# The low half of each weight block by an accumulating transfer instead of a subtraction

## The chip, the cores and the metric

The kernel runs on one core of a Trainium2 chip. The metric is device time in microseconds (us) of one execution. The kernel before takes 1822.1 us, the median of two runs (1822.0 and 1822.19).

## The reference

Two layers of a transformer trunk on one sequence of 512 tokens with 1024 features, all in float32. A layer is a gated feed-forward block (width 2816), a mixer, and a second gated feed-forward block:

```python
for l in range(DEPTH):                                   # DEPTH = 2
    h = rms_norm(x, ffn1_norm[l])
    x = x + 0.5 * swiglu(h, ffn1_w_gate[l], ffn1_w_up[l], ffn1_w_down[l])
    h = rms_norm(x, mix_norm[l])
    proj = h @ w_in[l]                                   # q, k, v, u of 512 columns each
    ...                                                  # 4 heads of differential attention; 4 pooling groups
    x = x + jnp.concatenate([o, p], axis=-1) @ w_out[l]
    h = rms_norm(x, ffn2_norm[l])
    x = x + 0.5 * swiglu(h, ffn2_w_gate[l], ffn2_w_up[l], ffn2_w_down[l])
return rms_norm(x, final_norm)
```

Nearly all of the arithmetic is products of activations with weights that are used once per layer.

## The kernel before, in words

**Products in three parts.** Each float32 operand is held as two matmul-type (fp32r) tiles: a rounded "hi" and the remainder "lo". `mm3` (L84 to L87) makes one 128x128 by 128x512 product from three matmuls on TensorE: hi by hi (L85), hi weight by lo activation (L86), lo weight by hi activation (L87). The lo part of the weights is therefore first needed by the third matmul of a group.

**Weights.** `plan` lists all weight blocks in the order of use: 128 partitions by up to 2048 columns, up to 1 MB. `load_next` (L107) loads a block from DRAM by one transfer that SyncE's queue issues (L111) into `wraw`, of which there are two. Then `split` (L103) cuts it in halves ("tiles" below: 1024 columns each, 768 or 640 in the down projections, 256 for the pooling weights): ScalarE casts a tile to `whi` (L104), VectorE subtracts `whi` from `wraw` and writes `wlo` (L105). There are five `whi` and five `wlo` buffers; each is free again when TensorE has read the tile for the last time. `weights()` asks for the block behind the one about to be used. The first block of all goes another way: `first_project` (L612) loads it by rows and splits it in 128-column pieces.

**Order of the work.** Each engine runs its instructions in a fixed order that a scheduler has made from the program. TensorE runs through the projections of a feed-forward block in 1024-column tiles, 24 matmuls per tile (8 k tiles of three), then through the down projections (15 or 18 matmuls per tile), then the mixer, where steps of attention stand between quarters of projections. VectorE and ScalarE also carry the gating (`silu`, `up`, `hhi`, `hlo`), rope, softmax and the norms. GpSimd (POOL) only adds squares (`ssum`, L184, L201), raises to powers (`rT`, L231) and scales the rope tables (L370, L371).

Of the kernel before, what the change touches and what calls it, by code (L numbers as in the profile page):

```python
# [15 lines left out]
ALU = mybir.AluOpType  # L16
# [5 lines left out]
L = 2  # L22
# [10 lines left out]

# columns of the packed small parameters
C_F1 = 0
# [6 lines left out]

# columns of the constants that depend on shapes alone
K_COS = 0
# [4 lines left out]

# the dimensions of a head: those that rope pairs lie 16 apart in 32 partitions  # L50
ROPE_ORDER = np.arange(HD).reshape(2, 2, 16).transpose(1, 0, 2).reshape(-1)
ROPE_SWAP = [(i + 16) % 32 for i in range(32)]

# the quarters of the mixer's projections before which attention's and pooling's steps stand
S_AT = ((3, 4, 6, 8), (10, 11, 13, 15), (19, 20, 23, 25), (26, 26, 28, 29))
Y_AT = (23, 30)
# how many quarters behind their first part the others stand
LAG_Q, LAG_U, LAG_T, LAG_A, LAG_H, V_AT = 2, 2, 2, 3, 3, 14
# [3 lines left out]
def trunk(ctx: ExitStack, tc: tile.TileContext, xT, gu1, dn1, win_qk, win_v, win_u, poolw, wout, gu2, dn2, small, lams, consts, outT):  # L62
    nc = tc.nc
# [24 lines left out]

# [1 line left out]
    plan = []  # L90
# [10 lines left out]
    loaded = []  # L101

    def split(hi, lo, raw):  # L103
        nc.scalar.copy(hi, raw)  # L104
        nc.vector.tensor_sub(lo, raw, hi.bitcast(F32))  # L105

    def load_next(i):  # L107
        src, part = plan[i]
        n = src.shape[-1]
        raw = wpool.tile([P, WSLOT], F32, name="wraw", bufs=2)  # L110
        nc.sync.dma_start(raw[:, :n], src)  # L111
        parts = []
        for o in range(0, n, part):
            hi = wpool.tile([P, 1024], F32R, name="whi", bufs=5)
            lo = wpool.tile([P, 1024], F32R, name="wlo", bufs=5)
            split(hi[:, :part], lo[:, :part], raw[:, o : o + part])
            parts.append((hi, lo))
        loaded.append(parts)

    used = [0]  # L120

    def weights():
        """The next block of weights; the one behind it is loaded."""
        i = used[0]
        used[0] += 1
        while len(loaded) < min(i + 2, len(plan)):
            load_next(len(loaded))
        return loaded[i]

    # the tensor engine's clock rises with its load: it works until the first data are there  # L130
    warm = cpool.tile([P, P], BF16, name="warm")
# [4 lines left out]

# [1 line left out]
    x = cpool.tile([P, KD, S], F32, name="x")  # L138
# [9 lines left out]
    nc.vector.memset(ones, 1.0)  # L148
    # the table of functions comes in before the first data
    early = sml.tile([P, 1], F32, name="early", bufs=1)  # L150
# [4 lines left out]
    class Norm:  # L155
        """x * gain split in two, tile by tile, and the sum of the squares."""

# [31 lines left out]
    class Final:  # L189
        """x * gain in place, and the sum of the squares."""  # L190

# [26 lines left out]
    def rms_cols(sq, inv_n, tiles=range(4), pin=False):  # L218
        """1 / sqrt(mean of the squares over the partitions): tokens on the partitions."""
        ps = bank("ps_ms")  # L220
        for t in tiles:
            mm = nc.tensor.matmul(ps[:, t : t + 1], sq[:, t * P : (t + 1) * P], ones[:, 0:1], start=True, stop=True)
            if pin and t == tiles[0]:
                in_order(mm)
        return rsqrt_mean(ps, inv_n, slice(tiles[0], tiles[-1] + 1))
# [8 lines left out]
    def rms_rows(rT, tiles=range(4)):  # L234
        """The same, for all tokens on every partition."""
        n = len(tiles)
        ts = slice(tiles[0] * P, (tiles[-1] + 1) * P)
        b = single("rb")
        nc.vector.tensor_copy(b[:, ts].rearrange("p (t c) -> p t c", t=n), rT[:, tiles[0] : tiles[-1] + 1].unsqueeze(2).broadcast_to([P, n, P]))
        ps = bank("ps_r")  # L240
        for t in tiles:
            nc.tensor.transpose(ps[:, t * P : (t + 1) * P], b[:, t * P : (t + 1) * P], ident)
        r = single("r")
        nc.scalar.copy(r[:, ts], ps[:, ts])
        return r
# [7 lines left out]
    def project(norm, done):  # L253
        """Two column tiles of a projection of the normed x; yields between quarters."""
        parts = weights()
        for i in range(2):
            ps = bank("ps_pr")
            hi, lo = parts[i]
            for k in range(KD):
                c = slice(k * P, (k + 1) * P)  # L260
                mm3(ps, hi[:, c], lo[:, c], *norm.k(k), k == 0, k == KD - 1)
                if k == 3:
                    yield
            done(i, ps)
            yield
# [5 lines left out]
    def ffn(norm, l, nxt, first=None):  # L271
# [3 lines left out]
        def gated():  # L275
            """silu(gate) * up of the column tiles that stand in PSUM, split in two."""
            while r is not None and todo:
                j, i, ps = todo.pop(0)
                if i == 0:
                    s = single("silu")  # L280
                    nc.vector.tensor_mul(s, ps, r)  # L281
                    nc.scalar.activation(s, s, AF.Silu)  # L282
                    st[j] = s
                    continue
                u = single("up")
                nc.vector.tensor_mul(u, ps, r)  # L286
                if j % 2 == 0:
                    hh.append(arena("hhi"))
                    hl.append(arena("hlo"))
                hi, lo = hh[-1][:, j % 2, :], hl[-1][:, j % 2, :]  # L290
                nc.vector.tensor_mul(u, u, st.pop(j))  # L291
                nc.scalar.copy(hi, u)  # L292
                nc.vector.tensor_sub(lo, u, hi.bitcast(F32))  # L293

        st = {}
        for hf, (j0, nj) in enumerate(HALVES):
            hh, hl = [], []
            for j in range(nj):

                def done(i, ps, j=j):  # L300
                    todo.append((j, i, ps))
                    gated()

                work = first(done) if first and r is None and j == 0 else project(norm, done)
                if r is None and j == 1:
                    # the norm's factors, while the projections go on
                    next(work)
                    next(work)
                    rT = rms_cols(norm.ssum, 1.0 / D, pin=True)
                    next(work)  # L310
                    r = rms_rows(rT)
                    gated()
                run(work)
# [11 lines left out]
            last = hf == 1 and isinstance(nxt, Final)  # L325
# [4 lines left out]
            if last:  # L330
                # the last two column tiles by halves of the tokens: the first half leaves under the second
                n = KD - 2
# [14 lines left out]
    def mix(norm, l, nxt):  # L347
        st = {}

        def qk_project(h):  # L350
            """Queries (scaled) and keys of a head, with rope."""
            sw, t = pair32("sw"), pair32("t")
# [24 lines left out]
        def qk_split(h, t):  # L377
            # per map, on the two halves of the partitions: queries (hi, lo) on keys (lo, hi), in turn for the maps
            qs, ks, kf = arena("qs"), arena("ks"), arena("kf")
# [10 lines left out]
        def v_project():  # L390
            """The values, with the tokens on the partitions."""
            parts = weights()
            parts = parts + weights()
# [25 lines left out]
        def scores(h, qt):  # L419
            """The two maps for 128 queries and their difference, before the division by the first map's sum."""  # L420
            q, k, kf = st["qk", h]
# [23 lines left out]
        def turn(h, qt):  # L445
            """That difference with the keys on the partitions."""
            a = st["a", h, qt]
# [10 lines left out]
        def attend(h, qt):  # L458
            """128 queries of a head's output, on the partitions, and the sum of their squares."""
            at = st["at", h, qt]  # L460
# [31 lines left out]
        def u_project(pair):  # L492
            dh, dl = arena("dhi"), arena("dlo")

            def done(i, ps):
# [12 lines left out]
                nc.vector.scalar_tensor_tensor(df, cur, 1.0 / w, u, ALU.mult, ALU.subtract)  # L508
                # the first tokens see fewer positions
                e = sml.tile([P, 16], F32, name="edge")  # L510
# [32 lines left out]
        def out_work():  # L543
            """The output projection: pool groups and heads in the order in which they are ready."""
            ps, parts = [], []
# [31 lines left out]

        # the steps of attention and pooling stand between the quarters of the projections
        events = []
# [32 lines left out]
    def first_project(done):  # L612
        """The first block: weights and x come in by rows, and are used as they come."""
        src = plan[0][0].rearrange("p (i k n) -> p i k n", i=2, k=KD)
# [30 lines left out]

    # -lam per layer, on every partition
    nlam, subg = [], []
# [111 lines left out]
```

## Time and profile before

| | |
|---|---|
| runs | 1822.0 and 1822.19 us, median 1822.1 |
| span of the profiled execution, first to last instruction | 1818.8 us |
| TensorE matmul / weight load busy | 1801.7 us (99%) / 1480.6 us (81%) |
| VectorE busy | 919.1 us (51%) |
| ScalarE busy | 630.0 us (35%) |
| GpSimd busy | 85.2 us (5%) |
| SyncE's DMA queue | 169.17 MB, 26.4% of the 16 DMA engines' span |

The page gives no time of its own for the profiled execution beside the span; the median of the runs is 3.3 us above the span. A matmul's busy time is modelled and overlaps that of the next one, so the pace of TensorE is read from the distance between starts. "Idle before, releaser" names what an engine waited for. A transfer's time to landing runs from its issue to its completion.

### The profile page before, as it was taken

The numbers are of one execution on the slowest core, as the hardware profiler recorded it, in microseconds if no ns is written. First come the engines' busy times: TensorE is split into PE (matmuls) and PEld (weight loads), VectorE is DVE, ScalarE is ACT, GpSimd is POOL, SyncE is SP. The second block draws the span as 40 slices with busy tenths as digits, with TensorE's granted clock in tenths as the row PEclk, the third lists the DMA queues.
The fourth block names the chain that finished last, engine by engine and source line by source line (L and its number), as shares of the span: only waits on it lengthen the run. The fifth ranks groups of instructions, "written<-read, shape, count | busy, mean of one in ns | idle before, by whom it ended". The sixth has DMA issues, their size and how long they took to land.

```text
span 1818.8 us, 19923 instructions
## 1 busy us (share of the span) xinstructions
PE 1801.7 (99%) x8152; PEld 1480.6 (81%) x8152; DVE 919.1 (51%) x1350; ACT 630.0 (35%) x975; POOL 85.2 (5%) x66
## 2 busy tenths in 40 slices
PE   8999999999999999999999999999999999999997
PEld 7888888877788888888888888888777888888886
DVE  6443344477975443444444434444779644434433
ACT  6222232445553322222432222324445433222232
POOL 0000000110020000000100000002000200000001
PEclk9999999999999999999999999999999999999999
DMA  6222321322122222322322232223122222232221
GB/s 228 93 76 90 116 110 61 105 92 73 49 93 96 111 72 96 113 93 73 123 106 93 70 116 98 102 64 131 47 73 73 96 96 104 70 121 93 86 85 62
DMA packets 31805, 170.48 MB, mean 94 GB/s; under 512 B 3425, under 2 KB 8033, under 8 KB 17505
## 3 DMA queue, kind: packets, MB, share of 16 engines
q1 hardware_dynamic: 31568, 169.17, 26.4%
q8 instruction: 64, 1.05, 0.2%
q14 instruction: 29, 0.23, 0.0%
q10 hardware_dynamic: 144, 0.03, 0.0%
HBM read 167.09 MB, written 2.10 MB: 93 GB/s over the span
## 4 chain that ended last, share of the span: by engine, by line
PE 96%; DVE 2%; issue 1%; SPq 1%; DMA 0%; POOL 0%; ACT 0%; POOLq 0%; DVEq 0%; ACTq 0%
PE ps_pr L85 19%; PE ps_pr L87 19%; PE ps_pr L86 19%; PE ps_dn L86 9%; PE ps_dn L85 9%; PE ps_dn L87 9%; PE ps_wo L85 2%; PE ps_wo L87 2%; PE ps_wo L86 2%; PE ps_s L430 1%; PE ps_s L431 1%; PE ps_v L85 1%; PE ps_v L87 1%; PE ps_v L86 1%; PE ps_o L466 1%
## 5 line engine op out<-in xcount | busy, mean ns | idle before, releaser
L104 ACT CAST whi<-wraw 128x1024 fp32r<-128x1024 f32 (+4 forms) x370 | 338.5, 919 | 939.0 <-PE ps_pr L86 409.3
L85 PE MATMUL ps_pr<-xhi,whi 128*128 128x512 f32 x1600 | 626.8, 392 | 3.0 <-ACT whi L104 3.0
L87 PE MATMUL ps_pr<-xhi,wlo 128*128 128x512 f32 x1600 | 623.2, 389 | 0.5 <-DVE wlo L105 0.5
L86 PE MATMUL ps_pr<-xlo,whi 128*128 128x512 f32 x1600 | 622.9, 389 | 0.0
L105 DVE TENSOR_TENSOR wlo<-wraw,whi 128x1024 fp32r<-128x1024 f32 (+4 forms) x370 | 396.3, 1074 | 185.9 <-ACT whi L104 185.7
L85 PEld LDWEIGHTS ps_pr<-xhi,whi 128*128 128x128 f32 x1600 | 300.7, 188 | 65.5 <-ACT whi L104 4.2
L87 PEld LDWEIGHTS ps_pr<-xhi,wlo 128*128 128x128 f32 x1600 | 300.3, 188 | 63.9 <-DVE wlo L105 1.0
L86 PEld LDWEIGHTS ps_pr<-xlo,whi 128*128 128x128 f32 x1600 | 300.5, 188 | 61.3 <-DVE xlo L174 0.6
L85 PE MATMUL ps_dn<-hhi,whi 128*128 128x512 f32 (+1 forms) x724 | 277.5, 383 | 0.0
L87 PE MATMUL ps_dn<-hhi,wlo 128*128 128x512 f32 (+1 forms) x724 | 277.4, 383 | 0.0
L86 PE MATMUL ps_dn<-hlo,whi 128*128 128x512 f32 (+1 forms) x724 | 277.4, 383 | 0.0
L286 DVE TENSOR_TENSOR up<-ps_pr,r 128x512 f32<-128x512 f32 x88 | 60.8, 691 | 274.3 <-PE ps_pr L87 274.3
L85 PEld LDWEIGHTS ps_dn<-hhi,whi 128*128 128x128 f32 x724 | 136.1, 188 | 26.8
L86 PEld LDWEIGHTS ps_dn<-hlo,whi 128*128 128x128 f32 x724 | 136.1, 188 | 26.6
L87 PEld LDWEIGHTS ps_dn<-hhi,wlo 128*128 128x128 f32 x724 | 136.1, 188 | 26.6
L281 DVE TENSOR_TENSOR silu<-ps_pr,r 128x512 f32<-128x512 f32 x88 | 60.8, 691 | 174.2 <-PE ps_pr L87 171.0
L323 DVE SCALAR_TENSOR_TENSOR x<-ps_dn,x 128x512 f32<-128x512 f32 (+1 forms) x66 | 44.6, 676 | 137.1 <-PE ps_dn L87 137.1
L184 POOL TENSOR_TENSOR ssum<-ssum,sq 128x512 f32<-128x512 f32 x35 | 53.5, 1529 | 1048.5 <-ACT sq L181 1048.1
L292 ACT CAST hhi<-up 128x512 fp32r<-128x512 f32 x88 | 54.8, 624 | 76.0 <-DVE up L291 76.0
L293 DVE TENSOR_TENSOR hlo<-up,hhi 128x512 fp32r<-128x512 f32 x88 | 60.2, 687 | 17.2 <-ACT hhi L292 17.2
L291 DVE TENSOR_TENSOR up<-up,silu 128x512 f32<-128x512 f32 x88 | 60.5, 690 | 6.2 <-ACT whi L104 0.5
L282 ACT ACTIVATE silu<-silu 128x512 f32<-128x512 f32 x88 | 55.2, 628 | 3.6 <-DVE silu L281 2.9
(118 smaller groups left out, 1104.3 us busy)
## 6 DMA issues: line engine op xcount, KB each, us to landing
wraw<-gu SPq DMA_DIRECT2D x87, 1024.0 KB, 4.8
wraw<-dn1a SPq DMA_DIRECT2D x16, 768.0 KB, 4.3
wraw<-dn2a SPq DMA_DIRECT2D x16, 768.0 KB, 4.3
wraw<-dn1b SPq DMA_DIRECT2D x16, 640.0 KB, 3.9
wraw<-dn2b SPq DMA_DIRECT2D x16, 640.0 KB, 3.8
wraw<-wqk SPq DMA_DIRECT2D x8, 1024.0 KB, 4.7
wraw<-wo SPq DMA_DIRECT2D x8, 1024.0 KB, 4.8
wraw<-wv SPq DMA_DIRECT2D x4, 1024.0 KB, 4.8
```

The source lines that it names most:

```text
L85: nc.tensor.matmul(out, a_hi, b_hi, start=start, stop=False)
L86: nc.tensor.matmul(out, a_hi, b_lo, start=False, stop=False)
L87: nc.tensor.matmul(out, a_lo, b_hi, start=False, stop=stop)
L104: nc.scalar.copy(hi, raw)
L105: nc.vector.tensor_sub(lo, raw, hi.bitcast(F32))
L184: (nc.vector if first else nc.gpsimd).tensor_add(self.ssum, self.ssum, sq)
L281: nc.vector.tensor_mul(s, ps, r)
L282: nc.scalar.activation(s, s, AF.Silu)
L286: nc.vector.tensor_mul(u, ps, r)
L291: nc.vector.tensor_mul(u, u, st.pop(j))
L292: nc.scalar.copy(hi, u)
L293: nc.vector.tensor_sub(lo, u, hi.bitcast(F32))
```

## The change

For every block but the first, the lo tile is no longer subtracted by VectorE. ScalarE multiplies the raw tile by -1 into `wlo`, which rounds it as the cast does, and GpSimd's queue issues a transfer that reads the same weights from DRAM once more and adds them to `wlo` in place. The cast to `whi` stands behind these two in the program. `split` remains for the first block. Comments are removed, and the kernel's lines behind L116 stand three lower.

```diff
         for o in range(0, n, part):
             hi = wpool.tile([P, 1024], F32R, name="whi", bufs=5)
             lo = wpool.tile([P, 1024], F32R, name="wlo", bufs=5)
-            split(hi[:, :part], lo[:, :part], raw[:, o : o + part])
+
+            nc.scalar.mul(lo[:, :part], raw[:, o : o + part], -1.0)
+            nc.gpsimd.dma_start(lo[:, :part], src[:, o : o + part], accum_op=ALU.add)
+            nc.scalar.copy(hi[:, :part], raw[:, o : o + part])
             parts.append((hi, lo))
```

The first place is ScalarE near the start, where the first whole blocks are split (`sq` are squares for the norm, `r` its factor). Before:

```order
L178 ACTIVATE ssum<-x 128x512
L181 ACTIVATE sq<-x 128x512 x3
L104 CAST whi<-wraw 128x1024 x2
L181 ACTIVATE sq<-x 128x512 x4
L104 CAST whi<-wraw 128x1024 x4
L244 COPY r<-ps_r 128x512
```

Now:

```order
L181 ACTIVATE ssum<-x 128x512
L184 ACTIVATE sq<-x 128x512 x3
L117 ACTIVATE wlo<-wraw 128x1024
L119 CAST whi<-wraw 128x1024
L117 ACTIVATE wlo<-wraw 128x1024
L119 CAST whi<-wraw 128x1024
L184 ACTIVATE sq<-x 128x512 x4
L117 ACTIVATE wlo<-wraw 128x1024
```

Each cast has a multiplication ahead of it, on the same engine.

The second place is ScalarE in the middle of a feed-forward block (`silu` and `hhi` belong to the gating). Before:

```order
L282 ACTIVATE silu<-silu 128x512
L104 CAST whi<-wraw 128x1024
L292 CAST hhi<-up 128x512
L104 CAST whi<-wraw 128x1024
L282 ACTIVATE silu<-silu 128x512
```

Now:

```order
L285 ACTIVATE silu<-silu 128x512
L119 CAST whi<-wraw 128x1024
L117 ACTIVATE wlo<-wraw 128x1024
L295 CAST hhi<-up 128x512
L119 CAST whi<-wraw 128x1024
L117 ACTIVATE wlo<-wraw 128x1024
```

Here the cast goes first and the multiplication follows it.

The third place is GpSimd, from its first work to the start of the first mixer. Before:

```order
masks.py:199 AFFINE_SELECT ident<-ident 128x128
L231 TENSOR_TENSOR rT<-ms,nhalf 128x4
L184 TENSOR_TENSOR ssum<-ssum,sq 128x512 x7
L231 TENSOR_TENSOR rT<-ms,nhalf 128x4
L370 TENSOR_TENSOR cosr<-cst,r 128x512
```

Now:

```order
masks.py:199 AFFINE_SELECT ident<-ident 128x128
L118 DMA wlo<-gu 128x1024 x4
L234 TENSOR_TENSOR rT<-ms,nhalf 128x4
L118 DMA wlo<-gu 128x1024 x18
L118 DMA wlo<-dn1a 128x768 x16
L118 DMA wlo<-gu 128x1024 x20
L118 DMA wlo<-dn1b 128x640 x9
L187 TENSOR_TENSOR ssum<-ssum,sq 128x512
L118 DMA wlo<-dn1b 128x640 x2
```

GpSimd's queue now holds 354 transfers, one per tile, among the additions and powers that it had.

## Rows read from the trace of the kernel before

**Rows 1.** The page's head and part 1: span, busy time, share, instructions.

```profile
span 1818.8 us, 19923 instructions
...
PE 1801.7 (99%) x8152; PEld 1480.6 (81%) x8152; DVE 919.1 (51%) x1350; ACT 630.0 (35%) x975; POOL 85.2 (5%) x66
```

**Rows 2.** Busy time by windows; the first line names the columns.

```profile
core 0: us, PE busy (x) PEld busy (x) DVE busy (x) ACT busy (x) POOL busy (x), PEclk, DMA share, GB/s
0.00:20.00 20.00, 15.90 (x82) 12.46 (x82) 12.16 (x34) 13.96 (x32) 0.70 (x6) 1.00 0.87 283
...
200.00:300.00 100.00, 100.00 (x443) 82.80 (x442) 44.50 (x53) 28.51 (x35) 0.00 (x0) 1.00 0.25 92
450.00:470.00 20.00, 18.73 (x93) 14.79 (x92) 18.51 (x48) 10.97 (x25) 3.00 (x2) 1.00 0.00 0
1340.00:1360.00 20.00, 19.45 (x105) 16.21 (x104) 16.32 (x39) 10.11 (x23) 3.00 (x2) 1.00 0.15 53
1360.00:1380.00 20.00, 19.28 (x90) 15.09 (x91) 19.41 (x45) 10.11 (x24) 0.00 (x0) 1.00 0.17 59
1800.00:1818.00 18.00, 8.83 (x70) 8.14 (x68) 7.94 (x18) 3.53 (x8) 1.40 (x2) 0.79 0.35 117
```

**Rows 3.** Part 4 of the page: the chain that ended last, by engine.

```profile
PE 96%; DVE 2%; issue 1%; SPq 1%; DMA 0%; POOL 0%; ACT 0%; POOLq 0%; DVEq 0%; ACTq 0%
```

**Rows 4.** Timeline of TensorE and ScalarE in the first output projection: start, us.

```profile
525.02 2.00 ACT L104 CAST whi<-wraw 128x1024 fp32r<-128x1024 f32 x2 [1.51 <-PE ps_wo L86]
...
526.87 0.39 PE L85 MATMUL ps_wo<-cath,whi 128*128 128x512 f32 x1
...
532.31 0.39 PE L85 MATMUL ps_wo<-cath,whi 128*128 128x512 f32 x1
...
532.77 0.39 PE L87 MATMUL ps_wo<-cath,wlo 128*128 128x512 f32 x1
```

**Rows 5.** Timeline of ScalarE's casts in the first layer's second down half.

```profile
322.48 0.73 ACT L104 CAST whi<-wraw 128x640 fp32r<-128x640 f32 x1 [2.66 <-PE ps_dn L86]
...
325.89 0.73 ACT L104 CAST whi<-wraw 128x640 fp32r<-128x640 f32 x1 [1.25 <-PE ps_dn L86]
...
329.28 0.73 ACT L104 CAST whi<-wraw 128x640 fp32r<-128x640 f32 x1 [2.66 <-PE ps_dn L86]
```

**Rows 6.** Groups of instructions by shape: count, busy us, mean ns, idle before, releaser.

```profile
L105 DVE TENSOR_TENSOR wlo<-wraw,whi 128x1024 fp32r<-128x1024 f32 x222 | 276.9, 1249 | 77.7 <-ACT whi L104 77.5
L105 DVE TENSOR_TENSOR wlo<-wraw,whi 128x768 fp32r<-128x768 f32 x64 | 61.3, 958 | 67.1 <-ACT whi L104 67.1
L105 DVE TENSOR_TENSOR wlo<-wraw,whi 128x640 fp32r<-128x640 f32 x64 | 52.5, 820 | 41.1 <-ACT whi L104 41.1
L105 DVE TENSOR_TENSOR wlo<-wraw,whi 128x256 fp32r<-128x256 f32 x4 | 1.6, 409 | 0.0
L104 ACT CAST whi<-wraw 128x1024 fp32r<-128x1024 f32 x222 | 232.7, 1052 | 585.7 <-PE ps_pr L86 299.8 <-issue 180.5 <-PE ps_dn L86 90.6
L184 POOL TENSOR_TENSOR ssum<-ssum,sq 128x512 f32<-128x512 f32 x35 | 53.5, 1529 | 1048.5 <-ACT sq L181 1048.1
```

**Rows 7.** Part 3 of the page: SyncE's DMA queue, packets, MB, share of engines.

```profile
q1 hardware_dynamic: 31568, 169.17, 26.4%
```

**Rows 8.** Transfers by line: count, KB each, median us from issue to landing.

```profile
wraw<-gu SPq DMA_DIRECT2D x87, 1024.0 KB, 4.8
wraw<-dn1b SPq DMA_DIRECT2D x16, 640.0 KB, 3.9
cst<-consts SPq DMA_DIRECT2D x1, 584.0 KB, 8.8
wraw<-pw SPq DMA_DIRECT2D x4, 128.0 KB, 2.0
```

**Rows 9.** Line 111's issues on SyncE's queue: minimum, median, maximum ns.

```profile
L111 SPq DMA_DIRECT2D wraw<-gu x87: 327/328/599, 10.6 to 1704.9; - x87
```

**Rows 10.** Timeline where TensorE first uses a whole block.

```profile
18.44 1.99 ACT L104 CAST whi<-wraw 128x1024 fp32r<-128x1024 f32 x2 [1.13 <-DMA wraw<-gu]
19.52 2.36 DVE L105 TENSOR_TENSOR wlo<-wraw,whi 128x1024 fp32r<-128x1024 f32 x2 [0.94 <-ACT whi L104]
...
20.80 0.50 PE L87 MATMUL ps_pr<-xhi,wlo 128*128 128x512 f32 x1 [0.53 <-DVE wlo L105]
```

## The prediction

> **What bounds the kernel now.** I read the page's head first. TensorE is busy 1801.7 of 1818.8 us; no other engine is above 51% [rows 1]. The windows then say where its 17.1 us of idle time lie. In a stretch of a feed-forward block, 200 to 300 us, TensorE has no gap at all; 4.1 us are lost in the first 20 us, 9.2 us in the tail from 1800 us, and some 2.5 us in three windows of the two mixers, where VectorE is busy 16.3 to 19.4 of 20 us [rows 2]. The chain of waits agrees: 96% TensorE, 2% VectorE [rows 3]. So VectorE, which the change relieves, bounds almost nothing.
>
> TensorE's pace is to be read from starts: in the output projection one 1024-column tile takes from 526.87 to 532.31, 5.44 us for 24 matmuls or 0.227 us each [rows 4]. A 640-column tile is 15 matmuls, 3.40 us, and the casts of that stretch indeed follow each other at 3.40 us (322.48, 325.89, 329.28), each ended by TensorE, not by a transfer [rows 5]. This is the row that matters most: the preparation of weights runs as far ahead as the five buffers let it, and then waits for TensorE. A new tile can be begun when TensorE leaves the oldest one, with four others still to be used: 4 x 5.44 = 21.8 us of cover for 1024-column tiles, 4 x 3.40 = 13.6 us for 640.
>
> **The change, part by part.** *Removed:* 222 + 64 + 64 + 4 = 354 subtractions of 276.9 + 61.3 + 52.5 + 1.6 = 392 us on VectorE [rows 6], which falls from 919 to 527 us. None of it stands before TensorE except in the mixer windows above. There at most the 2.5 us of idle time come back, and at least nothing, because ScalarE, which serves the same softmax steps, receives a multiplication nearly as long (1.05 for 1.25 us). I take half, -1.3 us.
>
> *Added on ScalarE:* 354 multiplications. They have the shapes of the casts, so I price them as casts: 222 x 1.05, 64 x 0.73 for 640 columns, and 64 x 0.89, midway, for 768: 337 us [rows 5, 6]. ScalarE goes from 630 to 967 us, 53%. In a feed-forward tile that is about one extra us in 5.44; its casts spend their time waiting for TensorE, so this is covered.
>
> *Added on the DMA engines:* the bytes of 354 tiles once more: 222 x 0.524 + 64 x 0.393 + 64 x 0.328 + 4 x 0.131 = 163 MB. The queue that moves 169.17 MB takes 26.4% of the engines [rows 7]; as plain loads the new ones would take 25.5%, together 52%. The trace has no accumulating transfer. From below it cannot be cheaper than a plain load of its size: 512 KB land in 3.4 us, between 128 KB in 2.0 and 640 KB in 3.9. From above I take the slowest landing of about this size, 584 KB in 8.8 us while other loads ran [rows 8]. The value that I use is 4.8 us, the row of a 1024 KB load, since 512 KB of weights and 512 KB of destination have to be read. The Trainium skill ("Collectives: The Full Stack", Part 3) says that a reducing transfer reads two sources per chunk and so runs at about half the rate of a copying one; by it, as an estimate, the new queue would take 51% rather than 25.5% of the engines, and the first tile below would come 1.4 us later than by the plain row. No run here shows it yet.
>
> *Added on GpSimd:* 354 issues. SyncE's queue spends 0.33 us on one (0.60 at most) [rows 9]; GpSimd's own additions take 1.53 us [rows 6]. Between these, 117 to 542 us on an engine that is busy 85: covered. Its queue runs in order, so a transfer behind an `ssum` addition waits for that addition, and this for the square and the finished down tile. In the down stage that addition belongs to a tile used two blocks before the one being prepared, whose own buffer is not free earlier, so nothing is late.
>
> *Moved waits.* The new chain for a tile is cast, multiplication, transfer. For 640 columns: 0.73 + 0.73 + 8.8 = 10.3 us at the upper bound, inside the 13.6 of cover; for 1024: 1.05 + 1.05 + 8.8 = 10.9 in 21.8. Hidden. `wraw` is now released by ScalarE rather than VectorE, at about the same time.
>
> Two places have less cover. *The first whole block:* it lands at 18.44; TensorE's first matmul with its lo tile starts at 20.80, held by the subtraction [rows 10]. Now the multiplication goes first: 18.44 + 1.05 + landing = 22.9, 24.3 or 28.3, thus +2.1, **+3.5** or +7.5 us. The second tile, multiplied by 21.6, lands at 26.4, before TensorE asks at 24.3 + 5.4. *The output projection:* its four early tiles are held until the last head is done. The cast at 525.02 waits for TensorE, and the lo tile is needed at 532.77 [rows 4]. Cast and multiplication end at 527.1; landing at 530.5, 531.9 or 535.9: 0, **0** or +3.1 us, once per layer.
>
> Sum: 1818.8 + 3.5 + 0 - 1.3 = 1821.0 us of span. The median of the runs is 3.3 us above the span, so 1824 us. Without any cost at the start and with all of the mixer's idle time back it would be 1819; with the upper bounds, 1822.1 + 7.5 + 2 x 3.1 = 1836.
>
> **Rivals.** *A: the DMA engines become the bound, slower.* If an accumulating byte costs m plain bytes, the share is 26.4% + 25.5% x m, which passes 100% at m = 2.9. Then the loads no longer keep ahead, ScalarE waits for `wraw` instead of for TensorE, and the time follows the share: m = 3 gives 1.029 x 1818.8 + 3.3 = 1875, m = 4 gives 1.284 x 1818.8 + 3.3 = 2339 us. For it: in the first 20 us, with plain loads alone, the engines reach 0.87 [rows 2]. Against it: reading twice as much explains m = 2, not 3.
>
> *B: GpSimd or the latency becomes the bound, slower.* If the time L from free buffer to landed tile exceeds the cover, five buffers give one tile per (L + use) / 5. At L = 17 us a 640-column tile comes every 4.08 instead of 3.40 us (64 x 0.68 = 44) and a 768-column one, 18 matmuls, every 4.22 instead of 4.08 (64 x 0.14 = 9): 1875. At L = 20 it is 64 x 1.28 + 64 x 0.74 = 129 us: 1951. The 2% are passed near L = 16.3. The same bound appears if GpSimd needs over 3.4 us per issue. For it: no row shows what such an issue costs, and the queue is in order. Against it: L is 10.3 with my upper landing.
>
> *C: the relief of VectorE is worth more than the start costs.* Then 1818 to 1822. A gain of over 2% is nearly excluded: TensorE's 1801.7 us of busy time and 3.3 us around the span make 1805, and 2% less than now is 1786.
>
> *D: the output changes but not the work.* That the transfers don't appear at all is excluded by the order of GpSimd's instructions.
>
> **Numbers.** The forecast, everything hidden but the start, 0.66; A 0.15; B 0.15; C 0.03; a larger gain 0.01. The predicted time is the first: 1824 us. The range begins at 1818, C's end, and reaches to 1930: it takes in the upper bounds (1836), A up to m = 3.1 and B up to about L = 19. Left out are A beyond (0.11), B beyond (0.07) and 0.02 below. 2% (1786 and 1858) is what a measurement here can tell: faster 0.01, same 0.69, slower 0.30.
>
> **What would show it.** Right: TensorE without a gap in the feed-forward stretches, ScalarE's instructions on `wlo` and `whi` still ended by TensorE, a DMA share of 50 to 80%, and one gap of some 3 us more near 20 us. Start wrong: `wlo`'s transfer from issue to landing other than 4.8 us. A: DMA share at 0.9 in the feed-forward windows, ScalarE waiting for `wraw`. B: TensorE waiting for `wlo` at L87 mostly in the 640- and 768-column stretches, with GpSimd's queue busy or its landings over 13 us. What would make the prediction wrong above all is the price of the accumulating transfer, the one thing that no row here shows.

## The result and the profile after

The changed kernel takes 1843.7 us, the median of runs from 1842.5 to 1844.9, against 1822.1 before: a ratio of 1.012, 95% interval 1.0091 to 1.015. It is slower by some 22 us: clear of the scatter, but within the 2% inside which the prediction speaks of the same time. Times here and below are medians; one execution each of two experiment kernels, of 4662 us (the plain copy, whose only trace this is) and 5683 us (the mixer alone), is left out. The profiled execution has a span of 1840.8 us, 22.0 more than before [rows 1].

The page of the changed kernel: span, busy times, the two DMA queues (packets, MB, share of the 16 engines' span) and the chain that ended last.

```profile
span 1840.8 us, 20900 instructions
...
PE 1810.7 (98%) x8152; PEld 1485.5 (81%) x8152; DVE 552.8 (30%) x996; ACT 918.3 (50%) x1329; POOL 385.3 (21%) x420
...
q0 software_dynamic: 50976, 163.08, 50.3%
q1 hardware_dynamic: 31568, 169.17, 30.4%
...
PE 92%; DMA 3%; DVE 2%; issue 1%; POOL 1%; SPq 0%; ACT 0%; POOLq 0%; DVEq 0%; ACTq 0%
```

VectorE lost 366 us of work and ScalarE gained 288, and neither moved the end. The new queue q0 takes 50.3% of the engines' span for about as many bytes as the old one, which took 26.4% before [rows 7] and takes 30.4% beside it. The chain has a new entry: 3% DMA, against 0% [rows 3].

Windows of the changed kernel, columns as in [rows 2]: the start, a feed-forward stretch, and the two output projections with what follows them.

```profile
20.00:40.00 20.00, 14.81 (x60) 11.72 (x61) 5.38 (x10) 14.33 (x18) 6.12 (x7) 0.75 1.00 254
200.00:300.00 100.00, 100.00 (x443) 82.81 (x442) 21.45 (x31) 45.88 (x53) 17.45 (x20) 1.00 0.89 199
530.00:570.00 40.00, 36.31 (x149) 29.29 (x148) 13.39 (x17) 27.35 (x35) 16.92 (x16) 0.91 0.81 198
1440.00:1460.00 20.00, 16.31 (x65) 12.99 (x65) 9.56 (x12) 15.48 (x22) 10.38 (x9) 0.91 0.82 194
```

From 200 to 300 us TensorE does the same 443 matmuls without a gap, although the DMA share rose from 0.25 to 0.89. Most of the loss is in the other three windows, and there the granted clock (PEclk) falls too. TensorE's waits name it (us in total, times, longest):

```profile
PE ps_wo L87 <- DMA wlo<-wo: 7.4, 2, 3.7
PE ps_pr L87 <- DMA wlo<-gu: 4.8, 1, 4.8
PE ps_pr L85 <- ACT whi L119: 2.7, 1, 2.7
```

Three waits for a lo tile in the whole program: one at the start and one in each output projection. The third row existed before, with 2.24 us, the wait for the first whole block's load:

```profile
19.54 0.50 PE L85 MATMUL ps_pr<-xhi,whi 128*128 128x512 f32 x1 [2.24 <-ACT whi L104]
```

TensorE runs the same 8152 matmuls, and but for some steps inside the two mixers in the same order. So the start of the n-th matmul after, less that of the n-th before, says where time was lost:

| place | lost, us |
|---|---|
| start, up to the 96th matmul of the gate and up projections | 7.4 |
| first output projection | 6.8 |
| second output projection | 5.5 |
| front of the second layer's mixer | 1.9 |
| all else, four feed-forward blocks included | 0.4 |
| sum | 22.0 |

The first output projection on the timeline of the changed kernel (start, us, engine):

```profile
532.67 1.05 ACT L119 CAST whi<-wraw 128x1024 fp32r<-128x1024 f32 x1 [1.51 <-PE ps_wo L86]
...
533.63 1.05 ACT L117 ACTIVATE wlo<-wraw 128x1024 fp32r<-128x1024 f32 x1
...
534.71 8.64 SPq L111 DMA_DIRECT2D wraw<-gu  x2
...
534.98 0.92 POOL L118 DMA_DIRECT2D wlo<-wo  x1 [8.05 <-ACT wlo L117]
...
542.90 0.79 PE L87 MATMUL ps_wo<-cath,wlo 128*128 128x512 f32 x1 [3.69 <-DMA wlo<-wo]
543.50 0.63 PE L85 MATMUL ps_wo<-cath,whi 128*128 128x512 f32 x1
543.92 0.63 PE L86 MATMUL ps_wo<-catl,whi 128*128 128x512 f32 x1
```

The chain is as forecast: cast, multiplication, issue (0.30 us after the multiplication's end), transfer. The transfer takes 542.90 - 534.98 = 7.9 us, and the multiplication's end also freed `wraw`, so that the next raw load starts 0.3 us before it, on the same engines. The matmuls behind the gap follow each other at 0.427 us instead of 0.227, until 549.03, and take 0.63 us against 0.39 [rows 4]; the granted clock from 543 to 549 us is 0.50, the lower of TensorE's two levels, 1.2 GHz. So the gap costs twice: 3.9 us of standing and 3.0 of slow matmuls. At the start and in the second output projection the slow matmuls cost 2.0 and 1.7 us; by this reading of the traces 6.7 of the 22 us are clock.

The start, where TensorE first uses a whole block:

```profile
18.30 1.06 ACT L117 ACTIVATE wlo<-wraw 128x1024 fp32r<-128x1024 f32 x1
...
19.67 1.03 POOL L118 DMA_DIRECT2D wlo<-gu  x1 [18.36 <-ACT wlo L117]
...
20.34 0.80 PE L85 MATMUL ps_pr<-xhi,whi 128*128 128x512 f32 x1 [2.67 <-ACT whi L119]
...
26.41 0.79 PE L87 MATMUL ps_pr<-xhi,wlo 128*128 128x512 f32 x1 [4.85 <-DMA wlo<-gu]
```

Here the transfer takes 6.7 us. Transfers by line (KB each, median us from issue to landing):

```profile
wraw<-gu SPq DMA_DIRECT2D x87, 1024.0 KB, 5.8
wlo<-gu POOLq DMA_DIRECT2D x174, 512.0 KB, 7.8
```

512 KB accumulated take longer than 1024 KB loaded, and the raw load slowed from 4.8 [rows 8] to 5.8 us.

### The profile page after: what moved, and what is told of

Its sections match the earlier page's. It is cut to its first block, busy times and chain, and to the rows that moved or that the text cites. A ratio compares the mean times of both kernels' runs of the same rounds, so it can differ in the third digit from the quotient of the medians.

```text
span 1840.8 us, 20900 instructions
## 1 busy us (share of the span) xinstructions
PE 1810.7 (98%) x8152; PEld 1485.5 (81%) x8152; DVE 552.8 (30%) x996; ACT 918.3 (50%) x1329; POOL 385.3 (21%) x420
## 3 DMA queue, kind: packets, MB, share of 16 engines
q0 software_dynamic: 50976, 163.08, 50.3%
q1 hardware_dynamic: 31568, 169.17, 30.4%
## 4 chain that ended last, share of the span: by engine, by line
PE 92%; DMA 3%; DVE 2%; issue 1%; POOL 1%; SPq 0%; ACT 0%; POOLq 0%; DVEq 0%; ACTq 0%
PE ps_pr L85 19%; PE ps_pr L87 19%; PE ps_pr L86 19%; PE ps_dn L86 8%; PE ps_dn L85 8%; PE ps_dn L87 8%; PE ps_wo L85 2%; PE ps_wo L87 1%; PE ps_wo L86 1%; DMA wraw<-wv 1%; PE ps_s L433 1%; PE ps_s L434 1%; DMA wlo<-wo 1%; PE ps_v L85 1%; PE ps_v L86 1%
## 5 line engine op out<-in xcount | busy, mean ns | idle before, releaser
L119 ACT CAST whi<-wraw 128x1024 fp32r<-128x1024 f32 (+2 forms) x354 | 335.0, 946 | 762.8 <-issue 335.0
L87 PE MATMUL ps_pr<-xhi,wlo 128*128 128x512 f32 x1600 | 624.0, 390 | 4.8 <-DMA wlo<-gu 4.8
L87 PEld LDWEIGHTS ps_pr<-xhi,wlo 128*128 128x128 f32 x1600 | 300.9, 188 | 68.6 <-DMA wlo<-gu 5.6
L117 ACT ACTIVATE wlo<-wraw 128x1024 fp32r<-128x1024 f32 (+2 forms) x354 | 336.3, 950 | 9.7 <-DMA wraw<-wqk 4.6
L118 POOL DMA_DIRECT2D wlo<-gu x174 | 151.9, 874 | 702.6 <-ACT wlo L117 684.2
L87 PE MATMUL ps_dn<-hhi,wlo 128*128 128x512 f32 (+1 forms) x724 | 277.4, 383 | 0.0
L87 PEld LDWEIGHTS ps_dn<-hhi,wlo 128*128 128x128 f32 x724 | 136.0, 188 | 26.7
L87 PE MATMUL ps_wo<-cath,wlo 128*128 128x512 f32 x128 | 52.0, 406 | 7.4 <-DMA wlo<-wo 7.4
```

The source lines that it names most:

```text
L87: nc.tensor.matmul(out, a_lo, b_hi, start=False, stop=stop)
L117: nc.scalar.mul(lo[:, :part], raw[:, o : o + part], -1.0)
L118: nc.gpsimd.dma_start(lo[:, :part], src[:, o : o + part], accum_op=ALU.add)
L119: nc.scalar.copy(hi[:, :part], raw[:, o : o + part])
```

## The experiments

Theory: the transfers are hidden wherever the five buffers run ahead; the 22 us are the latency of single transfers at the start and in the output projections, lengthened by a raw load beside them, and the lower clock behind each gap. Rivals: the DMA engines' load as a whole (A), GpSimd's queue in order (B), or ScalarE's extra work. All edits stand in `load_next`, unless said; each kernel was timed on the same chip as the kernel before, whose medians there were 1821.0 to 1822.1 us.

| edit | us | ratio to before, 95% |
|---|---|---|
| VectorE splits the first whole block | 1835.7 | 1.0068 to 1.0102 |
| ... the output projection's last two blocks | 1836.4 | 1.0065 to 1.0095 |
| ... both | 1828.4 | 1.0025 to 1.0055 |
| accumulate in the mixer alone | 1821.1 | 0.9989 to 1.0008 |
| plain copy instead of accumulation | 1831.8 | 1.0043 to 1.0076 |
| no raw loads beside it | 1834.0 | 1.0056 to 1.0086 |
| spare transfers, free to run ahead | 2174.6 | 1.1917 to 1.1964 |
| fill the start's gap | 1842.0 | 1.0101 to 1.0137 |
| accumulate in feed-forward blocks alone | 1829.5 | 1.0034 to 1.0064 |
| the same less three blocks behind the mixer | 1821.8 | 0.9991 to 1.001 |
| spare transfers that need the raw tile | 1873.1 | 1.0262 to 1.0296 |

**The start by VectorE.**

```diff
+            if i == 1:
+                split(hi[:, :part], lo[:, :part], raw[:, o : o + part])
+                parts.append((hi, lo))
+                continue
             nc.scalar.mul(lo[:, :part], raw[:, o : o + part], -1.0)
```

> Only the first whole block (the block behind the first) goes back to the cast and the subtraction; every other block keeps the accumulating transfer. My theory: of the 22 us that the change costs, 7.4 are lost there, because TensorE waits for one accumulating transfer and then runs at a lower clock for a while. It expects 7 us less than the changed kernel, about 1836.5 us, with TensorE's gap before its first whole block's L87 back under 1 us. Rival (ScalarE): the loss comes from the 354 multiplications in ScalarE's ordered queue, all along the program; then two multiplications fewer change less than 1 us. Rival (engines): the loss comes from the DMA engines being at 0.81 on average; then two transfers fewer change less than 1 us as well.

1835.7 us, as expected. The loss at the start falls from 7.4 to 1.5 us; the output projections keep 5.6 and 5.8 (and 1.2 us are lost at the front of the first mixer), with `PE ps_wo L87 <- DMA wlo<-wo: 7.6, 2, 3.9`.

**The output projection's last two blocks by VectorE**, the condition being

```diff
+            if i % 90 in (50, 51):
```

> Only the last two blocks of the output projection, in both layers, go back to the cast and the subtraction. My theory: 6.8 and 5.5 us are lost there in the two layers; expected 12 us less than the changed kernel, about 1831.5 us, and no wait of TensorE for wlo from wo. Both rivals (ScalarE's queue, DMA engines' load) expect 1842 to 1844 us, since 8 of 354 transfers are no more than 2% of either.

1836.4 us, 4.9 above what was expected; the runs range from 1832.8 to 1838.7, and the trace is of the fastest. The waits for `wlo<-wo` are gone, and nothing is lost inside the output projections. The start's wait was 6.8 us this time instead of 4.8, its loss 9.1: that one transfer's landing varies from run to run (8.2 us here). A further 1.4 us are lost just behind the first output projection. So the two places are separate.

**Both.**

```diff
+            if i == 1 or i % 90 in (50, 51):
```

> The two edits together: the first whole block and the last two blocks of each output projection go back to the subtraction; 344 of 354 tiles keep the accumulating transfer. My theory: the sum, about 19.5 us less than the changed kernel, 1824 us, within 2 to 3 us of the kernel before, with the share of the DMA engines still near 0.8. Rivals: 1840 us or more.

1828.4 us, where 1824 was expected. No matmul waits for a lo tile any more, though q0 still takes 48.8% of the engines. But 1.0025 to 1.0055 remain: 2.0 us at the start, 4.2 and 1.2 just behind the output projections, 2.1 before the second mixer. At the last three places TensorE waits for `xhi`, ScalarE's activation (2.5 us in three waits), which is taken up below.

**The mixer alone.** All other blocks are split by VectorE, those two of the output projection too.

```diff
+            if not 38 <= i % 90 < 50:
```

> Only the mixers' projections, pooling weights and the first two output blocks are made by the accumulating transfer; both feed-forward blocks and the last output blocks by the subtraction. My theory: neither the start nor the output projection waits, so it stands within 2 us of the kernel before, 1821 to 1824 us; less than 1822.1 only if VectorE's relief in the mixer is worth more than the 0.2 and 1.5 us by which the changed kernel's mixers came later. Rival (ScalarE): the mixers hold the densest work of ScalarE, so most of the loss would be there, 1830 us or more.

1821.1 us, the same as before. In its trace the mixers lose 0.0 to 0.3 us; nothing comes back there, although VectorE is busy 876.7 instead of 919.1 us. The 2.1 us that its span is longer lie at the start, whose code is that of before: a raw load landed 0.4 us later, and the matmuls from 22.0 to 25.0 us ran 0.427 us apart. The kernel before itself ranges from 1819.6 to 1823.0 us in these runs, so 2 us at the start of one trace can't be put down to an edit.

**A plain copy instead of the accumulation.** The lo tile is then the raw weights.

```diff
-            nc.gpsimd.dma_start(lo[:, :part], src[:, o : o + part], accum_op=ALU.add)
+            nc.gpsimd.dma_start(lo[:, :part], src[:, o : o + part])
```

> The transfer on GpSimd's queue stays where it is, but copies the weights over the tile instead of adding them (the low halves are then not the remainders: this part of the computation is changed). It has the same instructions on ScalarE and GpSimd and half of the reading. My theory: what counts is the landing of the transfer. I expect the new queue's share to fall from 50% to about 26%, the landing of a 512 KB transfer from 7.8 to 4.5 to 5.5 us, and the time to about 1830 us (start and output projection lose 2 to 3 us less each in idle time and some of the lower clock). Rival (ScalarE's queue): nothing changes, 1842 to 1844 us.

1831.8 us, 1.8 above what was expected: about half of the loss is the accumulation, and half is there with a plain second transfer of these bytes behind ScalarE and GpSimd. How long these transfers took to land in the runs of this time is not shown.

**No raw loads beside it.** Only the first whole block is loaded; all later tiles are made from that one.

```diff
-        raw = wpool.tile([P, WSLOT], F32, name="wraw", bufs=2)
-        nc.sync.dma_start(raw[:, :n], src)
+        raw = wkeep
+        if i == 1:
+            nc.sync.dma_start(raw[:, :n], src)
```

> The raw weights of the first whole block stay in a buffer of their own and are cast and negated for every later block; no later raw load is issued (so the hi halves and the negated halves of all later blocks are those of one block: this part is left out). The accumulating transfers are all there. My theory: a landing of 7 to 8 us is 4.8 us alone, plus the time that a raw load in flight takes from the same engines. I expect the new queue at 45 to 50% of the engines, a median landing of 4.5 to 5.5 us for 512 KB, and 1828 to 1832 us. If the landing stays at 7 us or more, the transfer is slow by itself and the collision is not the cause; then 1838 us or more.

1834.0 us, 2 above the range that was expected, as the landing and the queue's share are above theirs. Its queues, its landings and then TensorE's waits:

```profile
q0 software_dynamic: 50976, 163.08, 55.4%
q1 hardware_dynamic: 5936, 7.15, 1.2%
...
wlo<-gu POOLq DMA_DIRECT2D x174, 512.0 KB, 5.7
```

```profile
PE ps_wo L87 <- DMA wlo<-wo: 4.4, 3, 1.8
PE ps_pr L87 <- DMA wlo<-gu: 4.0, 1, 4.0
```

Alone, 512 KB accumulate in 5.7 us. So of the 7.8 about 2.1 come from sharing with the raw loads, and the longest wait in the output projections falls from 3.7 to 1.8 us. The rest of the gaps is the accumulating transfer's own latency. Nor is anything lost at the front of the second mixer here, where the changed kernel lost 1.9 us.

**Load, first try.** One more accumulating transfer per tile, into one of two spare tiles that nothing reads.

```diff
+            m = part * 192 // 1024
+            nc.gpsimd.dma_start(spare[len(spent) % 2][:, :m], src[:, o : o + m], accum_op=ALU.add)
```

> Beside each accumulating transfer GpSimd issues another one of 192/1024 of its size into a spare tile that nobody reads. Theory (engines are not the bound yet, but near it): the new queue's share goes from 50% to 60%, the mean to 0.9; in the feed-forward windows, where it was 0.89, it comes to 1.0, and the tiles' landing rises from 7.8 to some 10 us, still inside the cover of 21.8 and 13.6 us. I expect 1845 to 1860 us, the growth in the start and the output projections. If the engines already limit the feed-forward stretches, the time follows the share: 1843 x 1.1, about 2000 us.

2174.6 us, far outside of what was expected, and for another reason than the engines' load. The spare transfers depend on no tile, so the scheduler put all 354 of them into the first part of GpSimd's order; they were issued from 1.5 to 848 us. There each waits until an earlier one into the same tile has landed, and the transfers for `wlo` stand behind. GpSimd in that stretch:

```profile
307.85 0.88 POOL L125 DMA_DIRECT2D spare<-gu  x1 [2.92 <-DMA spare<-gu]
308.39 1.23 POOL L122 DMA_DIRECT2D wlo<-dn1a  x1
308.94 1.58 POOL L125 DMA_DIRECT2D spare<-gu  x1
314.53 0.87 POOL L125 DMA_DIRECT2D spare<-gu  x1 [4.01 <-DMA spare<-gu]
316.99 0.87 POOL L125 DMA_DIRECT2D spare<-gu  x1 [1.59 <-DMA spare<-gu]
317.53 1.23 POOL L122 DMA_DIRECT2D wlo<-dn1a  x1
```

A lo tile is issued every 6.8 to 9.9 us where one is used every 4.08 us (18 matmuls), while the DMA share of that stretch is only 0.75 to 0.78; from 900 us on, with no spare left, TensorE is busy 200.00 of 200 us. It is rival B, made by the experiment: a queue in order is bound by the waits in it, here at a lower DMA share than the changed kernel's 0.89.

**Load, second try.** The spare transfer now reads the raw tile in SBUF, and so can't run ahead.

```diff
+            nc.gpsimd.dma_start(spare[len(spent) % 2][:, :m], raw[:, o : o + m], accum_op=ALU.add)
```

> The changed kernel with one more accumulating transfer per tile, 192 of 1024 columns from the raw tile in SBUF into one of two spare tiles (its sum is used by nothing). Unlike the first load test it cannot run ahead, since it needs the raw tile. 18.75% more accumulated bytes: the new queue at 59 to 60% instead of 50.3%, the DMA share in a feed-forward window about 0.98 to 1.0 instead of 0.89; GpSimd 354 more issues of 0.87 us, 694 us in all. Theory (the engines have room left, latency counts only where TensorE waits): TensorE keeps its pace in the feed-forward stretches, the gaps at the start and at the two output projections grow by at most 1 to 3 us each, 1842 to 1855 us. Rival A (the DMA engines are already close to being the bound at 0.89): time goes with the share, the feed-forward stretches get 5 to 10% longer, over 1900 us. Rival B (GpSimd's queue in order): waits for the lo tile in the feed-forward stretches with GpSimd's queue waiting for the spare tiles, over 1870 us.

1873.1 us, above the 1842 to 1855 of the theory and in the range that was given to rival B. Page, window and TensorE's longest wait of this kernel:

```profile
q0 software_dynamic: 101952, 193.67, 60.1%
q1 hardware_dynamic: 31568, 169.17, 28.1%
```

```profile
200.00:300.00 100.00, 100.00 (x443) 82.83 (x442) 22.14 (x32) 47.17 (x54) 32.83 (x38) 1.00 0.96 218
```

```profile
PE ps_r L252 <- DVE rb L249: 12.1, 6, 3.4
```

At a DMA share of 0.96 the feed-forward stretch still has no gap, so rival A's loss does not appear at this load. How far off it is the share can't say: it adds up the times of packets, and in the changed kernel it is 1.06 from 1280 to 1286 us. What grew is what stands behind a wait in GpSimd's queue: rival B's mechanism, though not at the place that was named for it. Besides the gaps known (9.7 us at the start, 8.0 and 7.9 in the output projections), 7.6 us are lost at the front of the first mixer, 5.5 between the layers, 6.5 at the front of the second mixer, and 4.2 and 6.3 behind the two output projections, at the norms:

```profile
391.30 0.16 DVE L239 TENSOR_SCALAR ms<-ps_ms 128x4 f32<-128x4 f32 x1 [0.21 <-PE ps_ms L232]
...
393.38 1.80 POOL L125 DMA_DIRECT2D spare<-wraw  x2 [4.04 <-DMA spare<-wraw]
...
394.54 1.70 POOL L241 TENSOR_TENSOR rT<-ms,nhalf 128x4 f32<-128x4 f32 x1
...
396.27 0.43 DVE L249 COPY rb<-rT 128x512 f32<-128x512 f32 x1 [4.82 <-POOL rT L241]
```

The norm's power `rT` has its input at 391.5 and starts at 394.5, because GpSimd stands in front of it with a transfer that waits for an earlier one's landing.

**Filling the start's gap** with 44 small matmuls, to see what the clock is worth there (in the projection loop, for the second block's first product).

```diff
+                    for _ in range(44):
+                        in_order(nc.tensor.matmul(fill[:, :P], warm, warm, start=True, stop=True))
```

> In TensorE's gap at the start, between the second and the third matmul of the first whole block, 44 small matmuls of ones into a spare bank (about 4.7 us at full clock) that nobody waits for. They take no work away and the gap keeps its length. Theory (clock): part of the 7.4 us lost at the start is the lower clock behind the gap; with the filler the granted clock between 20 and 40 us stays at 1.0 instead of 0.75 and 2.5 to 3.5 us come back: about 1840.5 us. Rival: the clock fell for another reason; then 1843 to 1844 us and the clock still falls.

1842.0 us, within the scatter of the changed kernel. It didn't do its work: the lo tile landed 8.0 us after its issue this time, so 2.5 us of gap were left behind the fill, and the clock fell all the same, a little later:

```profile
21.32 4.25 PE L270 MATMUL ps_fill<-warm 128*128 128x128 bf16 x44
28.11 0.50 PE L271 MATMUL ps_pr<-xhi,wlo 128*128 128x512 f32 x1 [2.54 <-DMA wlo<-gu]
...
28.94 0.63 PE L87 MATMUL ps_pr<-xhi,wlo 128*128 128x512 f32 x1
```

Inconclusive on the price; that the slow matmuls follow the gaps is read from the traces alone.

**The feed-forward blocks alone.**

```diff
+            if i == 1 or 38 <= i % 90 < 52:
```

> Accumulating transfers only in the feed-forward blocks; the first whole block, the mixer's blocks and the output projection are split by VectorE as before. Bytes of the new queue: 163.1 less 25.7 (mixer) less 1.0 (first block) = 136 MB, so about 42% of the engines instead of 50.3%. Theory (the feed-forward stretches hide all of it): the 22 us vanish but for up to 2 us at the start, 1820 to 1826 us, no difference to before that a measurement tells. Rival (the 4 to 6 us that remained when both the start and the output projection were split by VectorE came from the feed-forward blocks, through ScalarE's or the DMA engines' load): 1826 to 1830 us.

1829.5 us: the rival's figure, not the theory's 1820 to 1826. But the place is not the rival's. The feed-forward stretches lose nothing; 1.7 us are lost at the start, and 4.1 and 2.5 us just behind the two output projections, where the norm's activations are made:

```profile
548.03 1.06 ACT L121 ACTIVATE wlo<-wraw 128x1024 fp32r<-128x1024 f32 x1 [5.73 <-DMA wraw<-gu]
...
551.84 0.71 ACT L180 ACTIVATE xhi<-x,sm 128x512 fp32r<-128x512 f32 x1
...
554.87 0.70 ACT L180 ACTIVATE xhi<-x,sm 128x512 fp32r<-128x512 f32 x1
...
555.63 0.50 PE L85 MATMUL ps_pr<-xhi,whi 128*128 128x512 f32 x1 [1.51 <-ACT xhi L180]
```

ScalarE stands 5.7 us with a multiplication whose raw load is late, and the two `xhi` activations behind it come when TensorE already wants them; slow matmuls follow. In the full change nothing is lost just behind the output projections; that the longer wait for `wlo` ahead of them covers this stall is likely, but not shown.

**The same, with the first three blocks behind the output projection split by VectorE.**

```diff
+            if i == 1 or 38 <= i % 90 < 55:
```

> As the kernel with accumulating transfers in the feed-forward blocks alone, and the first three weight blocks behind the output projection split by VectorE as well. That kernel lost 1.7 us at the start, 4.1 and 2.5 us just behind the two output projections, and nothing else. Theory (behind the output projection ScalarE, whose queue is in order, waits with a multiplication for a raw load, and the xhi activations that TensorE wants stand behind it; the load comes late beside the first accumulating transfers): with no such transfer there the 6.6 us go and the start stays, 1822 to 1825 us, feed-forward stretches at TensorE's pace. Rival (ScalarE's extra work or the engines' load costs a few us wherever a feed-forward block begins): the loss moves three blocks on, 1826 to 1830 us.

1821.8 us beside 1821.5: no difference, as the theory had it (1.4 us are lost at the start, 0.1 in all the rest). The head and a window of this kernel:

```profile
span 1820.3 us, 20768 instructions
...
PE 1804.0 (99%) x8152; PEld 1482.5 (81%) x8152; DVE 627.9 (34%) x1062; ACT 859.8 (47%) x1263; POOL 334.5 (18%) x354
```

```profile
200.00:300.00 100.00, 100.00 (x443) 82.81 (x442) 23.53 (x34) 45.85 (x54) 16.58 (x19) 1.00 0.88 198
```

130 MB are still accumulated, 40.6% of the engines' span, with 288 of the 354 multiplications on ScalarE, and none of it costs anything that the runs can tell. Nor does it gain: TensorE was the bound and stays it. No version beat the kernel before.

## Why the prediction was right, and where it was off

The forecast's case came: everything hidden but single places, and the time, 1844 us, lies in the range. But the forecast was 1824, some 2 us above the kernel before, and the loss was 22; even the upper bounds of that case made only 1836. The range held 1844 because it was drawn wide for rivals A and B, and neither came: so far it is luck. The path was right, and the price of the places on it was too low.

- *Feed-forward stretches: nothing.* Right. No loss in the trace, and shown by the last kernel's 0.9991 to 1.001. A sign that was given for rival A, a DMA share of 0.9 there, came without the loss (0.89): the share alone was no sign.
- *The price of the accumulating transfer: 4.8 us for 512 KB, taken from a raw load.* This is the step that failed. It measured 5.7 alone, 7.8 beside raw loads, 6.7 to 8.2 at the start. The row that I took had no other queue beside it; the upper row (8.8 us "while other loads ran") was the nearer one, and in the output projection the changed order of releases says why: the multiplication that starts the transfer also frees `wraw` and so starts a load. The Trainium skill ("DMA: Bandwidth & Descriptors", Queues, rings and completion order) says that each engine takes turns between the queues that have work, a packet at a time; the fall from 7.8 to 5.7 us without raw loads agrees.
- *The DMA share: 25.5% as plain loads, 51% by the rule of two reads.* It was 50.3%: 50.3 / 25.5 gives m = 1.97, and rival A's point, m = 2.9, was not reached. The Trainium skill gives this rule for reductions between cores ("Collectives: The Full Stack", Part 3); the trace of this transfer inside one core agrees with it. The share is no fixed price, though: without raw loads the same bytes took 55.4%.
- *The start: +3.5, bounds 2.1 to 7.5.* +7.4: the matmul at 26.4 instead of 24.3 us (0.3 for GpSimd's start, 1.9 for the landing), and 1.8 us of lower clock behind the gap, which had no term in the sum (the 2.0 above count a slow matmul ahead of that gap too).
- *The output projection: 0 per layer, bounds 0 to 3.1.* +6.8 and +5.5, above the bound, for three reasons. Landing 7.9 instead of 4.8. The lower clock, 3.0 and 1.7 us. And a row read wrongly: I put the tile's first use of lo at 532.77 [rows 4]. By the count of matmuls that row is the third k step's; the one that waits in the changed kernel is the 123rd of the output projection, which started at 531.41 before. The deadline was 1.4 us earlier than I wrote. (Nor does a tile begin at 526.87; the pace read from there, 24 matmuls in 5.44 us, holds.)

```profile
531.41 0.39 PE L87 MATMUL ps_wo<-cath,wlo 128*128 128x512 f32 x1
```

- *The mixer: -1.3.* 0 to +0.3, and 1.9 lost at the front of the second. There a cast of ScalarE waits 3.75 us for a raw load, and `xhi` behind it comes late: the relief of VectorE was worth nothing, and the transfers' load on the raw ones had no term in the sum.

```profile
1285.16 1.05 ACT L119 CAST whi<-wraw 128x1024 fp32r<-128x1024 f32 x1 [3.75 <-DMA wraw<-wv]
...
1287.08 0.71 ACT L176 ACTIVATE xhi<-x,sm 128x512 fp32r<-128x512 f32 x1
...
1288.62 0.50 PE L86 MATMUL ps_pr<-xlo,whi 128*128 128x512 f32 x1 [0.28 <-DVE xlo L177]
```

- *ScalarE 967 us, VectorE 527, GpSimd covered.* 918, 553, and 385. The multiplications took 336.3 us, as priced (337); instructions that overlap count once in an engine's busy time, so ScalarE's rose by less. An issue keeps GpSimd busy 0.87 us, between my bounds.

What stays open is the spread of the landing at the start (6.7, 8.0 and 8.2 us in three traces), and what the clock alone is worth there, since the fill failed.

## What to carry to other kernels

Work that runs ahead of the bound through several buffers was free here even at a DMA share of 0.96. Price a new transfer where the preparation has just been held up, at the start and behind a dependency, and price it there with the transfers that its own releases start beside it. Add to each new gap of TensorE the slow matmuls behind it, here 1.7 to 3.0 us for gaps of 4 to 5.5. On engines with a queue in order, look at what stands behind an instruction that may wait for a transfer: a norm's power was delayed by 3.1 us there, and activations came too late for TensorE.

## What the runs showed of the hardware

- A transfer that adds DRAM to SBUF took twice the engine time per byte of the plain loads before (50.3% of 1840.8 us for 163 MB, against 26.4% of 1818.8 for 169 MB); the plain loads beside it rose to 30.4%. And GpSimd was busy 0.87 us with each issue whether it carried 320 or 512 KB.
- A transfer's latency depended on its neighbours: 512 KB accumulated in 5.7 us without raw loads and in 7.8 us with them, and a raw load of 1024 KB took 4.8 us before the change and 5.8 beside the accumulating transfers.
- After gaps of 4 to 5.5 us between matmuls, TensorE ran 8 to 13 matmuls at the lower level (0.427 us apart instead of 0.227) before it was back. What followed shorter gaps differed between traces: at the start the lower level came behind 2.75 us in the mixer's kernel and did not come behind 2.63 us in the kernel before, so one trace can't price it.
